# Decoder layer in split fp32: low weight parts at another address, and all high products of a stage ahead of the low ones

## The chip, the cores and the metric

The kernel runs on one core of a Trainium2 chip. The time is device microseconds of one execution, from the chip's own measurement; three runs of the kernel before took 1108.66 to 1108.97 us, median 1108.82. Beside them stands one execution that the hardware profiler recorded; its page and its trace are what is quoted here as the profile. On the page PE is TensorE (matmul), PEld its weight loads, DVE is VectorE, ACT ScalarE, POOL GpSimd, SP SyncE, which issues most DMAs.

## What is computed

One layer of a decoder over 256 rows of 2048 columns in float32: normalise, project to queries, keys and values of sixteen heads of 128, attend (eight heads with stick-breaking, eight with rotary and dilated windows), normalise each head, project back, add; then normalise, project up to 11008 columns, convolve over three rows, gate with GELU, project down, normalise and add.

```python
h = rmsnorm(x, pre_mix_gain)
proj = jnp.einsum('bsd,de->bse', h, w_in)
q_sb, k_sb, v_sb, q_dl, k_dl, v_dl = jnp.split(proj, splits, axis=-1)
o_sb = stick_breaking_attention(q_sb, k_sb, v_sb)              # 8 heads
o_dl = dilated_attention(rope(q_dl), rope(k_dl), v_dl)         # 8 heads
mixed = concat(head_rmsnorm(o_sb, sb_out_gain), head_rmsnorm(o_dl, dil_out_gain))
x = x + rmsnorm(mixed @ w_out, post_mix_gain)
h = rmsnorm(x, pre_ffn_gain)
u = causal_depthwise_conv(h @ w_up, conv_w, width=3) + conv_b
gate, val = jnp.split(u, 2, axis=-1)
x = x + rmsnorm((gelu(gate) * val) @ w_down, post_ffn_gain)
```

## The kernel before

**Split operands.** [...] A product is then high × high, high × low and low × high. `load` (L73) brings a weight chunk of 128 x 2048 from HBM in two halves of 128 x 1024 (tag `raw`, five buffers), issued on SP; `high` (L86, ScalarE, L88) and `low` (L91, VectorE, L93) write `wh` and `wl`, four buffers each, that is two chunks' worth. `split` (L82) does both for a chunk. `ahead` (L184) keeps loads two chunks ahead of the matmuls and splits one chunk ahead.

**The chunks** (L166 to L180) run in this order: values (`v`), and per head a query and a key chunk (`qk`), the output projection (`out`), then 43 gate and 43 value chunks of the up projection (`up`). The loop at L738 takes one chunk a turn; a turn is called a stage here, and it ends with `step()` (L910), which moves every head under way on by one piece of its attention, and with `down.presum` (L912), whose argument is the tick.

**Products of a `qk` or `up` chunk** are in `mm_stationary` (L96). The weights are the stationary operand. For each of the two halves come eight matmuls of a high part, moving 512 columns of `hT2` (256 high and 256 low columns of the activations, L101), then eight of a low part, moving the 256 high columns (L104); so a chunk runs eight high, eight low, eight high, eight low, all into one PSUM tile. The first two `up` chunks have their own order (`mm_stationary_late`, L106). Values, output and down hold the activations stationary and move 512 columns of weights (`mm_moving`, L133, and `Down.multiply`, L607).

**After the products** of an `up` chunk `convolved` (L486) adds the PSUM halves, scales by row, convolves and gates on VectorE and ScalarE. A `qk` chunk is added to `qk` (L776) and then used by `stick_head` (L366) or `dilated_head` (L394), generators whose pieces `step` runs a stage apart: scores `z`, exponentials, `spl` (L384) or the rotated `qk` (L400), products, and `finish_head` (L334).

**Presums.** `Down.presum` (L563) sums pairs of blocks of the down weights ahead of time, one pair per two ticks: at an even tick it loads `b12` and `t13` (L578, L580), at the odd tick after the next, three later, VectorE adds them (L574), and a tick after that the sum is stored to HBM (L569). `t13` has three buffers. All three DMAs are issued on SP, between the raw loads.

**Addresses.** On-chip memory is given out per partition in program order of the pools. In the compiled kernel before, `hT`, `raw`, `wh`, `wl`, `ident`, `x1`, `mix`, `qk`, `cv`, `yt`, `yp` and nearly every other large tile begin 384 bytes past a multiple of 512; slices of them are taken at multiples of 512 bytes. Small tiles (a few columns) lie in the pool `small` in steps of 32 bytes.

**Order.** The instructions of each engine are laid out by the framework's planner from priorities, dependencies and free buffers, except where the kernel pins them (`pin`, `keep_in_program_order`). [...]

Of the kernel before, what the change touches and what calls it, by code (L numbers as in the profile page):

```python
# [9 lines left out]
F32 = mybir.dt.float32  # L10
# [3 lines left out]
ALU = mybir.AluOpType  # L14
# [37 lines left out]
def layer_kernel(ctx: ExitStack, tc: tile.TileContext, a, out: bass.AP):  # L52
# [15 lines left out]
            tc.keep_in_program_order(ins)  # L68
        return ins

    HALF = 1024

    def load(src, w, piece=HALF):  # L73
        raws = []
# [4 lines left out]
            raws.append(raw)  # L79
        return raws  # L80

    def split(raws):  # L82

        return [low(raw, high(raw)) for raw in raws]

    def high(raw):  # L86
        wh = wpool.tile([P, raw.shape[1]], F32R, tag="wh", name="wh", bufs=4, padded_shape=[P, HALF])
        pin(A.copy(wh, raw))  # L88
        return wh

    def low(raw, wh):  # L91
        wl = wpool.tile([P, raw.shape[1]], F32R, tag="wl", name="wl", bufs=4, padded_shape=[P, HALF])
        pin(V.tensor_tensor(wl, raw, wh.bitcast(F32), op=ALU.subtract))  # L93
        return wh, wl

    def mm_stationary(ps, parts, h):  # L96

        for i, (wh, wl) in enumerate(parts):
            for j in range(8):
                k = 8 * i + j  # L100
                T.matmul(ps, wh[:, j * P:(j + 1) * P], h[:, k, :, :], start=(k == 0), stop=False, skip_group_check=True)  # L101
            for j in range(8):
                k = 8 * i + j
                T.matmul(ps[:, 0, :], wl[:, j * P:(j + 1) * P], h[:, k, 0, :], start=False, stop=(k == KT - 1), skip_group_check=True)  # L104
# [45 lines left out]

    def rstd_of(v, n):

        l = small.tile([P, n], F32, tag=f"rl{n}", name="rl")
        A.activation(l, v, AF.Ln)
        r0 = small.tile([P, n], F32, tag=f"r0{n}", name="r0")
        A.activation(r0, l, AF.Exp, scale=-0.5)
        q = small.tile([P, n], F32, tag=f"rq{n}", name="rq")
# [3 lines left out]
        r = small.tile([P, n], F32, tag=f"rr{n}", name="rr")  # L161
        V.tensor_tensor(r, r0, q, op=ALU.mult)
        return r

# [19 lines left out]
    def ahead(i, splits=SPLITS):  # L184
        if i + LOADS >= len(chunks):
            down.load(2 * (i + 1 + LOADS - len(chunks)))
        if i + 1 == len(chunks):
            down.prepare(2)
        while len(raws) < min(len(chunks), i + 1 + LOADS):
            j = len(raws)  # L190
            if j in between:
                nc.sync.dma_start(*between[j])
            raws[j] = load(chunks[j][3], chunks[j][4])
        while len(parts_of) < min(len(chunks), i + 1 + splits):
            j = len(parts_of)
            parts_of[j] = split(raws[j])
        return parts_of[i]


# [8 lines left out]
    phA = tc.tile_pool(name="phA", bufs=2)  # L208
    apool = phA.__enter__()
    cst = apool.tile([P, C_END - P], F32, name="cst", bufs=1)  # L210
    gpre = small.tile([P, KT], F32, name="gpre", bufs=1)
    x1 = apool.tile([P, 2, D], F32, name="x1", bufs=1)
    x1_kept = nc.dram_tensor("x1_kept", (S, D), F32, kind="Internal").ap()

# [33 lines left out]
    def split_block(g, k):  # L248
        c = slice(k % 2 * 512, k % 2 * 512 + 512)
        if k % 2 == 0:  # L250
            first[g] = [wpool.tile([P, HALF], F32R, tag=tag, name=tag, bufs=4) for tag in ("wh", "wl")]
# [30 lines left out]
    for i in range(1, 4):  # L282
        load_x(4 * i, 4 * i + 4)
        for j in range(2 * i, 2 * i + 2):
            raws[j] = load(chunks[j][3], chunks[j][4])
        split_x(4 * i, 4 * i + 4)
        if i == 1:
            parts_of[2] = split(raws[2])
# [12 lines left out]
    sinR = apool.tile([P, 2, S], F32, name="sinR", bufs=1)  # L301
    rstd1 = cpool.tile([P, 2], F32, name="rstd1", padded_shape=[P, 2 + 112])

    def along_rows(r, name):

        ps = ps_at.tile([P, S], F32, tag="at", name=name)
        for t in range(2):
            dg = small.tile([P, P], F32, tag="diag", name="diag", bufs=1)
            V.tensor_scalar(dg, ident, r[t], -1.0, op0=ALU.mult, op1=ALU.mult)
            T.matmul(ps[:, t * P:(t + 1) * P], negones, dg, start=True, stop=True)  # L310
        return ps

    def first_norm():

        V.tensor_copy(tri, cst[:, C_TRI:C_TRI + P])
        G.tensor_copy(idb, ident)
        G.tensor_copy(mskb, cst[:, C_MSK:C_MSK + P])
        ss = small.tile([P, 2], F32, tag="ssx", name="ssx", bufs=1)
        for t in range(2):
            A.activation(gbc, x1[:, t, :], AF.Square, accum_out=ss[:, t:t + 1])  # L320
        v0 = small.tile([P, 2], F32, tag="vx", name="vx", bufs=1)
        V.tensor_scalar(v0, ss, 1.0 / D, EPS, op0=ALU.mult, op1=ALU.add)
        V.tensor_copy(rstd1, rstd_of(v0, 2))
        rps = along_rows((rstd1[:, 0:1], rstd1[:, 1:2]), "rps")
        V.tensor_scalar(rB[:, 0, :], rps, SCALE, None, op0=ALU.mult)
        V.tensor_copy(rB[:, 1, :], rps)
        for s in range(2):
            V.tensor_tensor(cosR[:, s, :], cst[:, C_COS:C_COS + S], rB[:, s, :], op=ALU.mult)
            V.tensor_tensor(sinR[:, s, :], cst[:, C_SIN:C_SIN + S], rB[:, s, :], op=ALU.mult)
# [4 lines left out]
    def finish_head(h, at, den):  # L334
# [4 lines left out]
        T.matmul(po[:, 0, :], at[:, 0:P], vt[:, 0, hc], start=True, stop=True)  # L339
        T.matmul(po[:, 1, :], at[:, P:2 * P], vt[:, 0, hc], start=True, stop=False)  # L340
        T.matmul(po[:, 1, :], at[:, 2 * P:3 * P], vt[:, 1, hc], start=False, stop=True)
        hs = small.tile([P, 2], F32, tag="hs", name="hs")
        for t in range(2):
            jk = apool.tile([P, P], BF16, tag="jk", name="jk")
            A.activation(jk, po[:, t, :], AF.Square, accum_out=hs[:, t:t + 1])
        v = small.tile([P, 2], F32, tag="hv", name="hv")
        if den is None:
            V.tensor_scalar(v, hs, 1.0 / P, EPS, op0=ALU.mult, op1=ALU.add)
        else:

            e2 = small.tile([P, 2], F32, tag="e2", name="e2")
# [42 lines left out]
    def dilated_head(h, qk):  # L394
# [9 lines left out]
        T.matmul(z[:, 0:P], qk[:, 0, 0:P], qk[:, 1, 0:P], start=True, stop=True)  # L404
        T.matmul(z[:, P:3 * P], qk[:, 0, P:S], qk[:, 1, :], start=True, stop=True)
        sm = apool.tile([P, 3 * P], F32, tag="t15", name="sm", bufs=3)
        m = small.tile([P, 2], F32, tag="m", name="m")
        den = small.tile([P, 2], F32, tag="den", name="den")
# [50 lines left out]
    def second_norm():  # L459

        rs = [sq.newton(*sq.mean(t)) for t in range(2)]
        r2B = cpool.tile([P, S], F32, name="r2B")
        V.tensor_scalar(r2B, along_rows(rs, "r2ps"), -0.5, None, op0=ALU.mult)
        return r2B


# [53 lines left out]
    class Down:  # L520
# [217 lines left out]
    for i, (kind, p, s, _, w) in enumerate(chunks):  # L738
# [40 lines left out]
        elif kind == "out":  # L779
# [14 lines left out]
            else:  # L794
# [40 lines left out]
                for t in range(2):  # L835
# [8 lines left out]
                    if t == 0:  # L844
                        for c in range(4):
                            update(0, c)
                        hs = [high(raw) for raw in raws[i + 1]]
                        up0.append(low(raws[i + 1][0], hs[0]))
# [12 lines left out]
                    highs(b)  # L861
                hs.append(high(raws[i + 2][1]))
                update(1, 3)
                up0.append(low(raws[i + 1][1], hs[1]))
                parts_of[i + 1] = up0
                for b in range(4, 6):
                    turn(1, b)
# [12 lines left out]
                square(1, 2, 3)  # L880
                lows(2)
                lows(3)
                parts_of[i + 2] = [low(raws[i + 2][0], hs[2])]
                for b in range(4, 8):
                    lows(b)
                parts_of[i + 2].append(low(raws[i + 2][1], hs[3]))
                parts_of[i + 3] = [low(raw, h) for raw, h in zip(raws[i + 3], hs[4:])]
                keep(0)
                keep(1)
                pinned[0] = False  # L890
# [102 lines left out]
```

## Time and profile before

| | before |
|---|---|
| median of three runs | 1108.82 us |
| the profiled execution | 1108.83 us |
| its span, first to last instruction | 1107.0 us |
| granted TensorE clock, mean | 0.997 |
| PE busy | 1095.9 us |
| PEld busy | 942.7 us |
| DVE busy | 879.1 us |
| ACT busy | 661.3 us |
| mean DMA rate | 233 GB/s |

The stretches of the span, read off the starts of the groups: values and query/key with the attention to about 304 us, the output projection and the second norm to about 400, up from 400 to 885, down from 885 on. In a row of the timeline stand the start, the time from there to the last end, engine, line, operation, out<-in, shape and count; neighbours of one kind are merged. In a row of groups stand the count, busy time and mean duration in ns of one, and the idle time before them. A matmul's duration is longer than its distance from the next, since matmuls are pipelined: distances are read from starts.

### The profile page before, as it was taken

To read this page: it belongs to the slowest core of one execution; us is meant where nothing else is said; L and a number is where in the kernel's file an instruction comes from. 1 tells how busy PE (TensorE), PEld (TensorE's weight loads), DVE (VectorE), ACT (ScalarE), POOL (GpSimd) and SP (SyncE) were. 2 spreads that over 40 slices of the span, in tenths; PEclk is the share of its full clock that TensorE was granted. 3 is DMA by queue.
4 is the path that set the end of the run, shared out by engine and by line. 5 is a ranking of instruction groups with operands and counts; after the bars stand their busy time and mean duration, and the time that the engine had idled before them with its cause. 6 is when DMAs were issued, how large, how long until landed. Compare 5 with 4: busy or idle time off the path is not lost.

```text
span 1107.0 us, 16307 instructions
## 1 busy us (share of the span) xinstructions
PE 1095.9 (99%) x5855; PEld 942.7 (85%) x5855; DVE 879.1 (79%) x1371; ACT 661.3 (60%) x1046; POOL 5.3 (0%) x12
## 2 busy tenths in 40 slices
PE   9999999999999999999999999999999999999996
PEld 6888888888888888888888888888888888888885
DVE  6577776777776589888888888888888898889887
ACT  6656664655654376656565555555556566666665
POOL 0000000000000000000000000000000000000001
PEclk9999999999999999999999999999999999999998
DMA  8977778878879856666555556556555577767775
GB/s 317 382 257 272 257 246 281 296 253 285 271 260 318 276 196 215 193 190 190 185 192 183 189 187 190 188 190 190 191 188 190 170 253 244 258 217 255 242 246 210
DMA packets 75393, 257.79 MB, mean 233 GB/s; under 512 B 8496, under 2 KB 9520, under 8 KB 74544
## 3 DMA queue, kind: packets, MB, share of 16 engines
q1 hardware_dynamic: 74880, 256.22, 69.5%
q8 instruction: 46, 0.75, 0.3%
q10 hardware_dynamic: 432, 0.53, 0.1%
q14 instruction: 35, 0.29, 0.1%
HBM read 238.89 MB, written 17.83 MB: 232 GB/s over the span
## 4 chain that ended last, share of the span: by engine, by line
PE 97%; DMA 1%; DVE 0%; ACT 0%; SPq 0%; issue 0%; DVEq 0%; ACTq 0%
PE mmu L101 28%; PE mmu L104 14%; PE mmqk L101 11%; PE p L622 7%; PE p L620 7%; PE p L621 7%; PE mmqk L104 6%; PE mmo L147 3%; PE mmo L143 3%; PE mmo L144 3%; PE mmv L147 2%; PE mmv L143 2%; PE mmv L144 2%; PE mmu L110 1%; DMA mg<-in_xT 1%; DMA raw<-in_w_v 0%
## 5 line engine op out<-in xcount | busy, mean ns | idle before, releaser
L88 ACT CAST wh<-raw 128x1024 fp32r<-128x1024 f32 (+1 forms) x408 | 414.6, 1024 | 348.3 <-PE mmu L101 186.6
L93 DVE TENSOR_TENSOR wl<-raw,wh 128x1024 fp32r<-128x1024 f32 (+1 forms) x408 | 482.3, 1188 | 159.2 <-ACT wh L88 147.9
L101 PE MATMUL mmu<-hT,wh 128*128 128x512 f32 x1344 | 336.8, 392 | 0.0
L101 PEld LDWEIGHTS mmu<-hT,wh 128*128 128x128 f32 x1344 | 241.7, 189 | 43.1
L104 PEld LDWEIGHTS mmu<-hT,wl 128*128 128x128 f32 x1344 | 183.4, 190 | 13.1
L104 PE MATMUL mmu<-hT,wl 128*128 128x256 f32 x1344 | 187.6, 282 | 0.0
L101 PE MATMUL mmqk<-hT,wh 128*128 128x512 f32 x512 | 131.7, 398 | 0.0
L101 PEld LDWEIGHTS mmqk<-hT,wh 128*128 128x128 f32 x512 | 92.2, 189 | 16.7
L104 PEld LDWEIGHTS mmqk<-hT,wl 128*128 128x128 f32 x512 | 69.8, 190 | 5.1
L104 PE MATMUL mmqk<-hT,wl 128*128 128x256 f32 x512 | 71.4, 282 | 0.0
L622 PE MATMUL p<-wl,yp 128*128 128x512 f32 x182 | 70.9, 390 | 0.0
L620 PE MATMUL p<-wh,yp 128*128 128x512 f32 x182 | 70.8, 389 | 0.0
L621 PE MATMUL p<-wh,yp 128*128 128x512 f32 x182 | 70.8, 389 | 0.0
L621 PE MATMUL p<-wh,yt 128*128 128x512 f32 (+1 forms) x140 | 53.6, 383 | 0.0
L620 PE MATMUL p<-wh,yt 128*128 128x512 f32 (+1 forms) x140 | 53.6, 383 | 0.0
L622 PE MATMUL p<-wl,yt 128*128 128x512 f32 (+1 forms) x140 | 53.4, 383 | 0.0
L493 ACT ACTIVATE cv<-u,par 128x256 f32<-128x256 f32 x86 | 51.4, 597 | 2.5 <-DVE u L491 2.3
L143 PE MATMUL mmv<-wh,hT 128*128 128x512 f32 x128 | 51.0, 400 | 0.0
L143 PE MATMUL mmo<-wh,mix 128*128 128x512 f32 x128 | 50.4, 394 | 0.0
L144 PE MATMUL mmv<-wh,hT 128*128 128x512 f32 x128 | 50.2, 392 | 0.2 <-DVE hT L228 0.2
L88 ACT CAST wh<-room 128x1024 fp32r<-128x1024 f32 x26 | 27.4, 1053 | 38.1 <-PE p L621 35.7
L144 PE MATMUL mmo<-wh,mix 128*128 128x512 f32 x128 | 49.8, 389 | 0.0
(178 smaller groups left out, 1221.2 us busy)
## 6 DMA issues: line engine op xcount, KB each, us to landing
raw<-in_w_up SPq DMA_DIRECT2D x172, 512.0 KB, 4.3
raw<-in_w_qk SPq DMA_DIRECT2D x64, 512.0 KB, 5.2
raw<-in_w_dn SPq DMA_DIRECT2D x60, 512.0 KB, 4.5
raw<-in_w_o SPq DMA_DIRECT2D x32, 512.0 KB, 5.1
raw<-in_w_v SPq DMA_DIRECT2D x28, 512.0 KB, 5.6
t<-in_w_dn SPq DMA_DIRECT2D x26, 512.0 KB, 5.7
t_kept<-t SPq DMA_DIRECT2D x26, 512.0 KB, 3.9
raw<-t_kept SPq DMA_DIRECT2D x26, 512.0 KB, 4.4
```

The lines of the kernel that those rows point to most:

```text
L88: pin(A.copy(wh, raw))
L93: pin(V.tensor_tensor(wl, raw, wh.bitcast(F32), op=ALU.subtract))
L101: T.matmul(ps, wh[:, j * P:(j + 1) * P], h[:, k, :, :], start=(k == 0), stop=False, skip_group_check=True)
L104: T.matmul(ps[:, 0, :], wl[:, j * P:(j + 1) * P], h[:, k, 0, :], start=False, stop=(k == KT - 1), skip_group_check=True)
L110: T.matmul(ps[:, part, :], parts[k // 8][low][:, k % 8 * P:(k % 8 + 1) * P], h[:, k, part, :], skip_group_check=True, **kw)
L143: T.matmul(ps[t], hi[:, k, tc_], ws, start=(first and i == 0 and j == 0), stop=False)
L144: T.matmul(ps[t], lo[:, k, tc_], ws, start=False, stop=False)
L147: T.matmul(ps[t], hi[:, k, tc_], wl[:, j * 512:(j + 1) * 512], start=False, stop=(last and i == len(parts) - 1 and j == n - 1))
L493: A.activation(cv, u, AF.Identity, scale=cw(2), bias=par[:, P_CB + f:P_CB + f + 1])
L620: T.matmul(ps, yh, wh[:, cs], start=key not in self.begun, stop=False)
L621: T.matmul(ps, yl, wh[:, cs], start=False, stop=False)
L622: T.matmul(ps, yh, wl[:, cs], start=False, stop=self.left[key] == 0)
```

## The change

- `low` takes the kind of the chunk. Each `wl` buffer is 512 bytes longer (`HALF + P` columns). For kinds `qk` and `up` the low part begins 80 columns, 320 bytes, into its buffer; for the others it begins at 0 as before. All `wl` buffers share a tag, so the four buffers still begin at the same place modulo 512.
- `mm_stationary` multiplies the high parts of both halves first, sixteen matmuls, then the low parts of both, sixteen. The products are the same ones.
- Small tiles of `rstd_of`, `finish_head` and `dilated_head` move from the pool `small` to the pool `apool`, with the same four buffers. `gpre` is padded by 128 bytes.
- `along_rows` takes its two diagonal matrices side by side in one tile from its caller (tag `half` of `apool` in the first norm, tag `pair` of `phB` in the second) in place of one `diag` tile used twice.
- `Down.presum` adds a pair at the even tick two after its loads, ahead of the next pair's loads, and stores it at the tick after that; `t13` has two buffers in place of three.

```diff
-    HALF = 1024
+    HALF, LOW_AT = 1024, 80
...
-    def low(raw, wh):
-        wl = wpool.tile([P, raw.shape[1]], F32R, tag="wl", name="wl", bufs=4, padded_shape=[P, HALF])
+    def low(raw, wh, kind=None):
+
+        at = LOW_AT if kind in ("qk", "up") else 0
+        wl = wpool.tile([P, at + raw.shape[1]], F32R, tag="wl", name="wl", bufs=4, padded_shape=[P, HALF + P])[:, at:]
         pin(V.tensor_tensor(wl, raw, wh.bitcast(F32), op=ALU.subtract))
         return wh, wl
 
     def mm_stationary(ps, parts, h):
 
-        for i, (wh, wl) in enumerate(parts):
+        for i, (wh, _) in enumerate(parts):
             for j in range(8):
                 k = 8 * i + j
                 T.matmul(ps, wh[:, j * P:(j + 1) * P], h[:, k, :, :], start=(k == 0), stop=False, skip_group_check=True)
+        for i, (_, wl) in enumerate(parts):
             for j in range(8):
                 k = 8 * i + j
                 T.matmul(ps[:, 0, :], wl[:, j * P:(j + 1) * P], h[:, k, 0, :], start=False, stop=(k == KT - 1), skip_group_check=True)
...
-        l = small.tile([P, n], F32, tag=f"rl{n}", name="rl")
+        l = apool.tile([P, n], F32, tag=f"rl{n}", name="rl", bufs=4)
...
-    gpre = small.tile([P, KT], F32, name="gpre", bufs=1)
+    gpre = small.tile([P, KT], F32, name="gpre", bufs=1, padded_shape=[P, KT + 32])
...
-    def along_rows(r, name):
+    def along_rows(r, name, dg):
 
         ps = ps_at.tile([P, S], F32, tag="at", name=name)
         for t in range(2):
-            dg = small.tile([P, P], F32, tag="diag", name="diag", bufs=1)
-            V.tensor_scalar(dg, ident, r[t], -1.0, op0=ALU.mult, op1=ALU.mult)
-            T.matmul(ps[:, t * P:(t + 1) * P], negones, dg, start=True, stop=True)
+            V.tensor_scalar(dg[:, t, :], ident, r[t], -1.0, op0=ALU.mult, op1=ALU.mult)
+            T.matmul(ps[:, t * P:(t + 1) * P], negones, dg[:, t, :], start=True, stop=True)
         return ps
...
-        rps = along_rows((rstd1[:, 0:1], rstd1[:, 1:2]), "rps")
+        dg = apool.tile([P, 2, P], F32, tag="half", name="diag", bufs=1)
+        rps = along_rows((rstd1[:, 0:1], rstd1[:, 1:2]), "rps", dg)
...
-        hs = small.tile([P, 2], F32, tag="hs", name="hs")
+        hs = apool.tile([P, 2], F32, tag="hs", name="hs", bufs=4)
...
-        V.tensor_scalar(r2B, along_rows(rs, "r2ps"), -0.5, None, op0=ALU.mult)
+        dg = phB.tile([P, 2, P], F32, tag="pair", name="diag", bufs=1, padded_shape=[P, 7, P])
+        V.tensor_scalar(r2B, along_rows(rs, "r2ps", dg), -0.5, None, op0=ALU.mult)
...
-            if not odd and 0 <= pair - 2 < len(self.presums):
-                t13, _, kept = self.summed[pair - 2]
+            if odd and 0 <= pair - 1 < len(self.presums):
+                t13, _, kept = self.summed[pair - 1]
                 tc.keep_in_program_order(nc.sync.dma_start(kept, t13))
-            if odd and 0 <= pair - 1 < len(self.presums):
+            if not odd and 0 <= pair - 1 < len(self.presums):
                 t13, one, _ = self.summed[pair - 1]
...
-                t13 = apool.tile([P, HALF], F32, tag="t13", name="t13", bufs=3)
+                t13 = apool.tile([P, HALF], F32, tag="t13", name="t13", bufs=2)
```

More of the change, by code (lines that the diff above doesn't have):

```diff
@@ L80, in load, with split @@
         return raws
-    def split(raws):
-        return [low(raw, high(raw)) for raw in raws]
+    def split(raws, kind):
+        return [low(raw, high(raw), kind) for raw in raws]
     def high(raw):
@@ L151, in rstd_of @@
     def rstd_of(v, n):
-        l = small.tile([P, n], F32, tag=f"rl{n}", name="rl")
+        l = apool.tile([P, n], F32, tag=f"rl{n}", name="rl", bufs=4)
         A.activation(l, v, AF.Ln)
-        r0 = small.tile([P, n], F32, tag=f"r0{n}", name="r0")
+        r0 = apool.tile([P, n], F32, tag=f"r0{n}", name="r0", bufs=4)
         A.activation(r0, l, AF.Exp, scale=-0.5)
-        q = small.tile([P, n], F32, tag=f"rq{n}", name="rq")
+        q = apool.tile([P, n], F32, tag=f"rq{n}", name="rq", bufs=4)
         V.tensor_tensor(q, r0, r0, op=ALU.mult)
@@ L160, in rstd_of @@
         V.tensor_scalar(q, q, -0.5, 1.5, op0=ALU.mult, op1=ALU.add)
-        r = small.tile([P, n], F32, tag=f"rr{n}", name="rr")
+        r = apool.tile([P, n], F32, tag=f"rr{n}", name="rr", bufs=4)
         V.tensor_tensor(r, r0, q, op=ALU.mult)
@@ L195, in ahead @@
             j = len(parts_of)
-            parts_of[j] = split(raws[j])
+            parts_of[j] = split(raws[j], chunks[j][0])
         return parts_of[i]
@@ L250, in split_block @@
         if k % 2 == 0:
-            first[g] = [wpool.tile([P, HALF], F32R, tag=tag, name=tag, bufs=4) for tag in ("wh", "wl")]
+            first[g] = [wpool.tile([P, HALF], F32R, tag=tag, name=tag, bufs=4, padded_shape=[P, n]) for tag, n in (("wh", HALF), ("wl", HALF + P))]
         wh, wl = (w[:, c] for w in first[g])
@@ L287, in layer_kernel @@
         if i == 1:
-            parts_of[2] = split(raws[2])
+            parts_of[2] = split(raws[2], chunks[2][0])
     tc.keep_in_program_order(nc.sync.dma_start(ident, a["cst"][:, C_ID:C_END]))
@@ L345, in finish_head @@
             A.activation(jk, po[:, t, :], AF.Square, accum_out=hs[:, t:t + 1])
-        v = small.tile([P, 2], F32, tag="hv", name="hv")
+        v = apool.tile([P, 2], F32, tag="hv", name="hv", bufs=4)
         if den is None:
@@ L349, in finish_head @@
         else:
-            e2 = small.tile([P, 2], F32, tag="e2", name="e2")
+            e2 = apool.tile([P, 2], F32, tag="e2", name="e2", bufs=4)
             V.scalar_tensor_tensor(e2, den, EPS, den, op0=ALU.mult, op1=ALU.mult)
@@ L406, in dilated_head @@
         sm = apool.tile([P, 3 * P], F32, tag="t15", name="sm", bufs=3)
-        m = small.tile([P, 2], F32, tag="m", name="m")
-        den = small.tile([P, 2], F32, tag="den", name="den")
+        m = apool.tile([P, 2], F32, tag="m", name="m", bufs=4)
+        den = apool.tile([P, 2], F32, tag="den", name="den", bufs=4)
         for t, cs in ((0, slice(0, P)), (1, slice(P, 3 * P))):
@@ L847, in layer_kernel @@
                         hs = [high(raw) for raw in raws[i + 1]]
-                        up0.append(low(raws[i + 1][0], hs[0]))
+                        up0.append(low(raws[i + 1][0], hs[0], "up"))
                         hs.append(high(raws[i + 2][0]))
@@ L863, in layer_kernel @@
                 update(1, 3)
-                up0.append(low(raws[i + 1][1], hs[1]))
+                up0.append(low(raws[i + 1][1], hs[1], "up"))
                 parts_of[i + 1] = up0
@@ L882, in layer_kernel @@
                 lows(3)
-                parts_of[i + 2] = [low(raws[i + 2][0], hs[2])]
+                parts_of[i + 2] = [low(raws[i + 2][0], hs[2], "up")]
                 for b in range(4, 8):
                     lows(b)
-                parts_of[i + 2].append(low(raws[i + 2][1], hs[3]))
-                parts_of[i + 3] = [low(raw, h) for raw, h in zip(raws[i + 3], hs[4:])]
+                parts_of[i + 2].append(low(raws[i + 2][1], hs[3], "up"))
+                parts_of[i + 3] = [low(raw, h, "up") for raw, h in zip(raws[i + 3], hs[4:])]
                 keep(0)
```

## The prediction

> **What bounds the kernel.** I read the page first: its span, its busy rows and its chain of work that ended last.
>
> ```profile
> span 1107.0 us, 16307 instructions
> PE 1095.9 (99%) x5855; PEld 942.7 (85%) x5855; DVE 879.1 (79%) x1371; ACT 661.3 (60%) x1046; POOL 5.3 (0%) x12
> ...
> PE 97%; DMA 1%; DVE 0%; ACT 0%; SPq 0%; issue 0%; DVEq 0%; ACTq 0%
> ...
> L101 PE MATMUL mmu<-hT,wh 128*128 128x512 f32 x1344 | 336.8, 392 | 0.0
> L104 PE MATMUL mmu<-hT,wl 128*128 128x256 f32 x1344 | 187.6, 282 | 0.0
> L101 PE MATMUL mmqk<-hT,wh 128*128 128x512 f32 x512 | 131.7, 398 | 0.0
> L104 PE MATMUL mmqk<-hT,wl 128*128 128x256 f32 x512 | 71.4, 282 | 0.0
> ```
>
> TensorE carries 97% of the chain, so a change is worth what it does to the spacing of matmuls. The edited function issues the last four groups. A stage is 16 high matmuls of 512 columns and 16 low ones of 256, now in the order 8, 8, 8, 8. There are 1344/16 = 84 stages in up and 512/16 = 32 in query/key, **116** in all, with 116 × 16 = **1856** low matmuls. The profiled execution took 1108.83 us, 1.8 us more than its span, and the median of the three runs is 1108.82, so the sum holds for both.
>
> The next view is the PE timeline of one stage in up; the first column is the start.
>
> ```profile
> 501.97 2.00 PE L101 MATMUL mmu<-hT,wh 128*128 128x512 f32 x8
> 503.81 1.12 PE L104 MATMUL mmu<-hT,wl 128*128 128x256 f32 x8
> 504.76 2.00 PE L101 MATMUL mmu<-hT,wh 128*128 128x512 f32 x8
> 506.61 1.11 PE L104 MATMUL mmu<-hT,wl 128*128 128x256 f32 x8
> 507.56 2.00 PE L101 MATMUL mmu<-hT,wh 128*128 128x512 f32 x8
> 509.40 1.12 PE L104 MATMUL mmu<-hT,wl 128*128 128x256 f32 x8
> 510.35 0.86 PE L101 MATMUL mmu<-hT,wh 128*128 128x512 f32 x3
> ```
>
> Ends are modelled, so I use starts. Eight highs take 1.84, 1.85 and 1.84 us (mean 1.843), eight lows 0.95 each time, a stage 507.56 − 501.97 = 5.59. Narrower windows of the same timeline give the spacing inside a run of lows (the first row starts with the second low, the next with the seventh), then the down stage, whose matmuls are all 512 wide and listed singly.
>
> ```profile
> 503.93 0.40 PE L104 MATMUL mmu<-hT,wl 128*128 128x256 f32 x2
> 504.52 0.40 PE L104 MATMUL mmu<-hT,wl 128*128 128x256 f32 x2
> 949.73 0.39 PE L621 MATMUL p<-wh,yp 128*128 128x512 f32 x1
> ...
> 952.90 0.39 PE L620 MATMUL p<-wh,yp 128*128 128x512 f32 x1
> ```
>
> From the second low to the seventh are five spacings in 0.59, and from the seventh to the next run (504.76) two in 0.24: **0.12 us** each. The first low takes 0.11 to 0.12 (503.81 to 503.93); by the run's total it is 0.95 − 7 × 0.12 = 0.11. The down stage has 14 spacings in 3.17: **0.2264** for a steady 512-column matmul. Eight steady ones would take 1.811, so a run of highs that follows lows loses 1.843 − 1.811 = 0.032 at its start.
>
> A steady 0.12 for 256 columns and 0.2264 for 512 differ by 0.106, which is what 256 columns cost; the remainder, 0.013 to 0.014, is paid once per matmul in both. One weight load runs beside each matmul in both, and in the addresses of the compiled kernel both streams, `hT` and weights, begin 384 bytes past a multiple of 512. So the remainder may be a collision of the two reads, and it depends on their phase: the first lows and first highs of a run differ from the later ones with the same addresses.
>
> **The order of the products.** One run of 16 and 16 loses one start of highs (0.032) and one short first low (0.01). Highs: 1.843 + 8 × 0.2264 = 3.654. Lows: 0.95 + 8 × 0.12 = 1.91. Together 5.564 against 5.587, 0.023 less, times 116 = **2.6 us** gained, certain as far as the rows go.
>
> **The address of the low parts.** No row of before has the two reads 320 bytes apart, so the steady low is bounded from both sides. [...]
>
> ```profile
> 203.81 0.49 PE L418 MATMUL ptw<-ident,sm 128*128 128x128 f32 x3
> L418 PE MATMUL ptw<-ident,sm 128*128 128x128 f32 x24 | 3.9, 272 | 0.0
> ```
>
> Three in 0.49 with 0.272 for one: (0.49 − 0.272) / 2 = **0.109**, 0.011 under the steady low. Above, by the worst spacing of highs. These are the second and the seventh high of the run that begins at 504.76, and the durations of all lows in up.
>
> ```profile
> 505.00 0.62 PE L101 MATMUL mmu<-hT,wh 128*128 128x512 f32 x2
> 506.15 0.62 PE L101 MATMUL mmu<-hT,wh 128*128 128x512 f32 x2
> L104 PE MATMUL mmu<-hT,wl x1344: 277/283/364, 413.7 to 881.7; 128*128 128x256 f32 x192
> ```
>
> The six spacings before the seventh take 506.15 − 504.76 = 1.39, 0.2317 each, 0.0053 over the steady ones; the first alone is 505.00 − 504.76 = 0.24, some 0.01 over. A bad phase thus costs 0.005 on average and 0.01 at worst, and the low could go to 0.125, at the extreme to 0.13. Between 0.109 and 0.13 I take **0.113**. Minimum and median of that last row are 277 and 283 ns: the shortest low lies 6 ns under the usual one (0.12 − 0.006 = 0.114), and by starts the first low of a run was 0.11. That is a phase which these matmuls have shown, and the steady 0.12 is nearly the worst they show. A stage is then 3.654 + 16 × 0.113 = 5.462, 0.125 less than now; times 116 is **14.5 us**, and 1108.8 − 14.5 = **1094.3**.
>
> [...]
>
> **What else is edited.** Who waits for whom, of PE, ACT and DVE, the busy times of the up stage, and the DMAs of the presums, from issue to landing:
>
> ```profile
> PE idle L236 <- DVE warm L233: 1.2, 1, 1.2
> ACT wh L88 <- PE mmu L101: 186.6, 164, 1.7
> DVE diag L309 <- PE rps L310: 3.6, 1, 3.6
> 412.00:885.00 473.00, 473.00 (x2707) 415.92 (x2706) 395.05 (x650) 280.46 (x424) 0.00 (x0) 1.00 0.59 190
> t<-in_w_dn SPq DMA_DIRECT2D x26, 512.0 KB, 5.7
> t_kept<-t SPq DMA_DIRECT2D x26, 512.0 KB, 3.9
> ```
>
> TensorE's longest wait of the whole run is 1.2 us, at the start, and casts wait for TensorE to free buffers, not the reverse. So the second `wh`, now needed eight lows (0.95) earlier, comes in time. VectorE works 395.05 of 473 us there (83.5%); if that stretch shrinks like the stage, by 0.125/5.587, to 462, it is at 85.5% and still not the bound. The copy of row `[128, 2, 128]` in place of one reused `diag` removes DVE's 3.6 us wait; TensorE was not held by it, so nothing. The presum's add moves one tick (one stage) earlier: its operand has two ticks, 10.9 us, and lands in 5.7. Its store is issued at the next odd tick, and with two buffers instead of three the load that reuses the buffer comes one tick, 5.46, after it; the store lands in 3.9. On SP the raw loads queue behind that load, with 1.5 us to spare before they are late, and ACT's casts, which wait for TensorE, hide that. If the cover were gone, 24 reuses at up to 1 us each could show, which I count as unlikely. The tiles moved between pools change only addresses: nothing.
>
> **Rivals.**
>
> *The floor*: the collision vanishes and lows run at 0.109. The stage is 3.654 + 1.744 = 5.398, 0.189 less, 21.9 us: **1086.9**. [...]
>
> *No effect of the address*: the remainder is a fixed price of these matmuls. Only the order counts: 1108.8 − 2.6 = **1106.2**. For it speaks that the remainder is equal at 256 and 512 columns; against, that the first low has less of it.
>
> *Low buffers come free later*: the first `wl` buffer of a stage is released after 24 products instead of 16. A DVE queue that keeps its order would stand at that `wl`, and attention operands behind it would reach TensorE late. Two places of the query/key stage, DVE first, PE after:
>
> ```profile
> 152.25 1.23 DVE L93 TENSOR_TENSOR wl<-raw,wh 128x1024 fp32r<-128x1024 f32 x1
> 153.40 0.55 DVE L384 TENSOR_TENSOR spl<-sp,sph 128x384 fp32r<-128x384 f32 x1
> 155.11 0.33 PE L387 MATMUL z<-spl,tri 128*128 128x384 f32 x1
> 208.22 1.22 DVE L93 TENSOR_TENSOR wl<-raw,wh 128x1024 fp32r<-128x1024 f32 x1
> 209.36 0.68 DVE L400 TENSOR_TENSOR qk<-qk,rot 128x512 f32<-128x512 f32 x1
> 210.40 0.39 PE L404 MATMUL z<-qk 128*128 128x128 f32 x2
> 204.06 2.09 PE L101 MATMUL mmqk<-hT,wh 128*128 128x512 f32 x8
> 149.04 2.09 PE L101 MATMUL mmqk<-hT,wh 128*128 128x512 f32 x8
> 150.97 1.11 PE L104 MATMUL mmqk<-hT,wl 128*128 128x256 f32 x8
> ```
>
> The stage that starts at 149.04 would free that buffer at 149.04 + 1.93 + 1.81 + 0.90 = 153.68; `wl` and `spl` then end near 155.46, and TensorE wants `spl` at about 154.98: 0.5 us late. By the same sum from 204.06, the start of its stage, `qk` is done at 210.6 and wanted at 210.27: 0.3 late. Eight heads of each kind: 8 × 0.5 + 8 × 0.3 = 6.4 us given back, **1100.7**. It needs the low part to stay ahead in DVE's order, which is laid out anew.
>
> *Slower: a worse phase.* If 320 bytes apart costs the lows what the first highs pay, 0.0053, they run at 0.1253; the stage is 3.654 + 2.005 = 5.659, 0.072 more, 8.4 us: **1117.2** (1126 at 0.13). It decides from (5.587 − 3.654) / 16 = 0.1208 on: a steady low above that makes the kernel slower. For it speaks that all reads now share one residue and the first highs show phases that cost more; against, that lows have not shown one clearly above 0.12.
>
> **How the numbers follow.** Main case 0.38, floor 0.18, no effect 0.16, late buffers 0.10, worse phase 0.18. The measurement tells about 0.2% (2.2 us) from no change. The main case, the floor and the late buffers are faster by more; 1106.2 lies at that border, half to each side: faster 0.74, same 0.08, slower 0.18. The range leaves out only the worse phase: from 1084 (floor, and the 0.023 per stage lost at a run's start gone a second time) to 1108 (the address nothing, and the order a third of its sum). Forecast **1094.3**.
>
> **What would show it.** In the PE timeline of the changed kernel a run of 16 highs should take 3.65 us, and 16 lows 1.81; 1.74 means the floor, 1.91 no effect, 2.0 a worse phase. Late buffers would show as PE waits on DVE at `spl` or `qk` and DVE waits of `wl` on PE. The highs' spacing should stay 0.2264; if it moves, the low parts' address also touches the run after them and the sum is wrong by up to 0.03 × 116 = 3.5 us.

## The result and the profile after

| | before | changed |
|---|---|---|
| median | 1108.89 us (4 runs, 1108.66 to 1109.27) | 1103.17 us (4 runs, 1102.63 to 1103.41) |
| ratio of the runs, 95% interval | | 0.9947 [0.9934, 0.9960] |
| span of the profiled execution | 1107.0 us | 1101.5 us |

The change gains 5.7 us, where 14.5 were forecast. The page of the changed kernel shows the same picture as before: TensorE carries the chain, and the two groups of `mm_stationary` in up (now L103 and L107) are its largest.

```profile
span 1101.5 us, 16267 instructions
PE 1089.8 (99%) x5855; PEld 940.5 (85%) x5855; DVE 872.3 (79%) x1371; ACT 668.0 (61%) x1046; POOL 5.3 (0%) x12
...
PE 96%; DMA 1%; ACT 1%; DVE 0%; issue 0%; SPq 0%; DVEq 0%; ACTq 0%
...
L103 PE MATMUL mmu<-hT,wh 128*128 128x512 f32 x1344 | 320.7, 391 | 0.0
L107 PE MATMUL mmu<-hT,wl 128*128 128x256 f32 x1344 | 172.4, 281 | 0.0
```

The PE timeline of the changed kernel, in up, is the view that answers to the one of before; the first column is the start.

```profile
499.79 3.81 PE L103 MATMUL mmu<-hT,wh 128*128 128x512 f32 x16
503.44 2.05 PE L107 MATMUL mmu<-hT,wl 128*128 128x256 f32 x16
505.33 3.81 PE L103 MATMUL mmu<-hT,wh 128*128 128x512 f32 x16
508.98 2.05 PE L107 MATMUL mmu<-hT,wl 128*128 128x256 f32 x16
510.87 3.81 PE L103 MATMUL mmu<-hT,wh 128*128 128x512 f32 x16
```

Sixteen highs take 503.44 − 499.79 = 3.65 us, as the sum had it. Sixteen lows take 505.33 − 503.44 = 1.89, **0.118 each**, where 1.81 and 0.113 were forecast. A stage is 5.54 instead of 5.587; 0.047 × 116 stages = 5.4 us, beside 5.5 between the spans. The product takes up's stage for those of query/key too. From the starts of the first matmul of each stretch in the two traces, the query/key stretch is 1.9 us shorter and the up stretch, from its third chunk on, 3.8 (84 × 0.047 = 3.9). So the gain lies in these two stretches, and nearly the whole miss in one number, the spacing of a low.

The last view of the changed kernel is who waits for whom: PE's longest two waits, two of DVE's, and one of SP's queue (us in total, times, longest).

```profile
PE idle L239 <- DVE warm L236: 1.2, 1, 1.2
PE pth L824 <- DVE x L816: 1.2, 1, 1.2
...
DVE wl L95 <- PE mmqk L107: 8.6, 13, 0.7
DVE wl L95 <- PE mmu L107: 5.4, 28, 0.8
...
SPq L584 <- DMA t_kept<-t: 42.7, 23, 3.7
```

VectorE does now wait for low buffers that TensorE frees later, and SP does wait for the store of a presum before it reloads the buffer, 42.7/23 = 1.9 us each time on average. Neither reaches TensorE: its waits are those of before, but for one of 0.4 us on an operand of the first projection.

### The profile page after: what moved, and what is told of

It reads as the page before. It is cut to its first block, busy times and chain, and to the rows that moved or that the text cites. A ratio compares the mean times of both kernels' runs of the same rounds, so it can differ in the third digit from the quotient of the medians.

```text
span 1101.5 us, 16267 instructions
## 1 busy us (share of the span) xinstructions
PE 1089.8 (99%) x5855; PEld 940.5 (85%) x5855; DVE 872.3 (79%) x1371; ACT 668.0 (61%) x1046; POOL 5.3 (0%) x12
## 4 chain that ended last, share of the span: by engine, by line
PE 96%; DMA 1%; ACT 1%; DVE 0%; issue 0%; SPq 0%; DVEq 0%; ACTq 0%
PE mmu L103 28%; PE mmu L107 14%; PE mmqk L103 11%; PE p L626 7%; PE p L625 7%; PE p L624 7%; PE mmqk L107 5%; PE mmo L147 3%; PE mmo L146 3%; PE mmo L150 3%; PE mmv L150 2%; PE mmv L146 2%; PE mmv L147 2%; DMA mg<-in_xT 1%; PE mmu L113 1%; DMA raw<-in_w_v 0%
## 5 line engine op out<-in xcount | busy, mean ns | idle before, releaser
L88 ACT CAST wh<-raw 128x1024 fp32r<-128x1024 f32 (+1 forms) x408 | 413.0, 1024 | 250.9 <-PE mmu L103 118.2
L95 DVE TENSOR_TENSOR wl<-raw,wh 128x1024 fp32r<-128x1024 f32 (+1 forms) x408 | 475.7, 1187 | 90.7 <-ACT wh L88 51.4
L103 PE MATMUL mmu<-hT,wh 128*128 128x512 f32 x1344 | 320.7, 391 | 0.0
L103 PEld LDWEIGHTS mmu<-hT,wh 128*128 128x128 f32 x1344 | 246.9, 188 | 47.7
L107 PEld LDWEIGHTS mmu<-hT,wl 128*128 128x128 f32 x1344 | 170.2, 189 | 6.4
L107 PE MATMUL mmu<-hT,wl 128*128 128x256 f32 x1344 | 172.4, 281 | 0.0
L103 PE MATMUL mmqk<-hT,wh 128*128 128x512 f32 x512 | 125.3, 396 | 0.0
L103 PEld LDWEIGHTS mmqk<-hT,wh 128*128 128x128 f32 x512 | 94.4, 188 | 18.9
L498 DVE SCALAR_TENSOR_TENSOR cv<-u,par,cv 128x255 f32<-128x255 f32 x86 | 41.6, 483 | 68.7 <-ACT cv L497 68.6
L107 PEld LDWEIGHTS mmqk<-hT,wl 128*128 128x128 f32 x512 | 64.8, 189 | 2.4
L107 PE MATMUL mmqk<-hT,wl 128*128 128x256 f32 x512 | 65.5, 281 | 0.0
L131 ACT COPY half<-mmu 128x256 f32<-128x256 f32 x86 | 32.0, 372 | 41.9 <-PE mmu L107 38.7
L88 ACT CAST wh<-room 128x1024 fp32r<-128x1024 f32 x26 | 27.4, 1053 | 38.8 <-PE p L625 37.0
```

Source lines behind the costliest of these rows:

```text
L498: V.scalar_tensor_tensor(cv[:, 1:], u[:, :S - 1], cw(1), cv[:, 1:], op0=ALU.mult, op1=ALU.add)
```

## The experiments

Every kernel below is the changed kernel with the edit shown. Spacings in ns are distances between the starts of neighbouring matmuls of one stage, read from the trace. Times of timed runs are medians, with the kernel before run on the same chip. A low and a high are a matmul of a low and of a high part: ScalarE writes the high part as an fp32r cast of the weights (`wh`, L88 of the changed kernel), VectorE the low part as the difference of weights and high part (`wl`, L95).

### The order alone, and the address alone

```diff
-    HALF, LOW_AT = 1024, 80
+    HALF, LOW_AT = 1024, 0
```

> The changed kernel with the low parts at the start of their buffers again, 0 bytes further; everything else of the change is kept. Theory A (both parts count: a run of highs after lows costs 0.027 us less often, and the other phase makes a low 0.118 instead of 0.120): lows steady at 0.120, 16 highs in 3.65 us, 1106.2 to 1106.6 us, 2.3 to 2.6 under before. Theory B (the order is the whole gain and the address does nothing): 1103.2, as the changed kernel.

Measured: **1106.18 us** (9 runs) beside 1108.81, ratio 0.9976 [0.9966, 0.9985]. Its PE timeline in up:

```profile
500.35 3.82 PE L103 MATMUL mmu<-hT,wh 128*128 128x512 f32 x16
504.00 2.08 PE L107 MATMUL mmu<-hT,wl 128*128 128x256 f32 x16
505.91 3.82 PE L103 MATMUL mmu<-hT,wh 128*128 128x512 f32 x16
```

Highs 3.65, lows 1.91: theory B falls, and the time is 2.6 us lower, to the tenth what the prediction's sum gave the order. In part that is luck: by the starts a stage in up takes 5.567 on average, 0.020 under before, which is 1.7 us over 84 stages; the rest is in the query/key stretch, 1.1 us shorter in the trace, whose stages also hold the attention's matmuls. The second kernel puts the order back:

```diff
-        for i, (wh, _) in enumerate(parts):
+        for i, (wh, wl) in enumerate(parts):
...
-        for i, (_, wl) in enumerate(parts):
             for j in range(8):
```

> The changed kernel with eight high, eight low, eight high, eight low again; the low parts stay 320 bytes further. Theory A: eight lows take 0.943 us instead of 0.952 (0.118 each, and the short first low of a run is gone), eight highs 1.84 as before: 2 x 0.009 x 116 = 2 us under before, 1106.9. Theory B: as before, 1108.9. A third outcome, 1104 or less, would say that the two parts help each other not at all and the address is nearly everything.

Measured: **1105.85 us** (8 runs) beside 1108.81, ratio 0.9973 [0.9962, 0.9983]. Its timeline:

```profile
500.63 2.00 PE L103 MATMUL mmu<-hT,wh 128*128 128x512 f32 x8
502.47 1.11 PE L106 MATMUL mmu<-hT,wl 128*128 128x256 f32 x8
503.41 2.00 PE L103 MATMUL mmu<-hT,wh 128*128 128x512 f32 x8
505.25 1.11 PE L106 MATMUL mmu<-hT,wl 128*128 128x256 f32 x8
506.19 2.00 PE L103 MATMUL mmu<-hT,wh 128*128 128x512 f32 x8
```

A stage is 506.19 − 500.63 = 5.56. The address alone gains 3.0 us, one more than expected (eight highs after these lows take 1.837 us, where before had 1.841, and eight lows 0.943 in place of 0.953). 2.6 and 3.0 make 5.6 beside the 5.7 of the whole change: the parts add up. Both kernels keep the moved tiles and the other presum order of the change, which no run tries by themselves; since they are in both sums, the sum of 5.6 leaves them about nothing. What is missing is missing in the address: 3.0 measured, 14.5 − 2.6 = 11.9 forecast.

### What sets the spacing of a low: the address?

```diff
-        at = LOW_AT if kind in ("qk", "up") else 0
+        at = 8 * (lows_at[0] // 2 % 16) if kind == "up" else 0
+        lows_at[0] += kind == "up"
```

> In up the low parts lie at another place in each chunk, 0, 32, 64 ... 480 bytes further in turn, in query/key at 0. Looked at is the steady spacing of the lows of each chunk. Theory A (collision of the two reads, which depends on their phase): the spacing differs by offset, 0.120 at 0, 0.118 at 320, and somewhere between 0.109 and 0.117. Theory C (a fixed price of some 0.011 us for each such matmul, the address moving it by a cycle or two only): 0.117 to 0.121 at every offset.

> In up the low parts lie 192, 196, 200 ... 252 bytes further in turn, in query/key 192. The coarse sweep had 0.1178 at 192 and 0.1168 at 224. Theory C2: every step stays between 0.1165 and 0.121, the best at 224 or beside it. A place under 0.114 would say that the collision can be dodged after all, and the fixed price falls.

The fine sweep has `at = 48 + lows_at[0] // 2 % 16`. Mean spacing of the lows in ns, by bytes of displacement (from the starts in the traces of the two runs, some 75 to 90 distances each, the first ones of a run included):

```
coarse   0: 119.7   32: 118.3   64: 117.7   96: 117.3  128: 120.4  160: 119.7  192: 117.8  224: 116.8
       256: 119.5  288: 118.3  320: 117.8  352: 117.3  384: 120.4  416: 119.7  448: 117.8  480: 116.8
fine   204: 122.6  208: 116.6  212: 117.3  216: 118.9  220: 121.1  224: 116.8  240: 117.3  252: 119.1
```

The pattern repeats every 256 bytes, not 512. Every place lies between 116.6 and 122.6, none near 109 or 113. At this point a fixed price of each such matmul (theory C) looked likely, though the fine sweep went beyond what C2 allowed (122.6 at 204, 121.1 at 220) and had its best place at 208, not at 224. The highs answer in the same way:

```diff
+        at = 8 * (highs_at[0] // 2 % 16) if kind == "up" else 0
+        highs_at[0] += kind == "up"
+        wh = wpool.tile([P, at + raw.shape[1]], F32R, tag="wh", name="wh", bufs=4, padded_shape=[P, HALF + P])[:, at:]
```

> Low parts at 0 everywhere; in up the HIGH parts lie 0, 32, 64 ... 480 bytes further in turn. Looked at is the spacing of highs of 512 columns by offset. Theory C2 (a fixed price of 0.010 us or more for each matmul, and 0.003 to 0.004 us that hang on the phase, as the sweep of the lows showed): 0.224 to 0.230, with the same repeat every 256 bytes. Theory D (highs have slack in the load, so that the address moves only the start of a run): 0.2264 at every offset.

Measured, mean spacing of highs including the start of a run: 228.5 at 0 and 228.9 at 192, 232.3 to 234.0 at the other places of this sweep, again with a repeat of 256 bytes. Theory D falls, and most places lie above the 224 to 230 of C2. None of these places is better for the highs than no displacement.

### Or the weight load?

In the next two kernels half of the weight columns are loaded, for highs and for lows in turn:

```diff
-                T.matmul(ps, wh[:, j * P:(j + 1) * P], h[:, k, :, :], start=(k == 0), stop=False, skip_group_check=True)
+                n = P if k == 0 else m
+                T.matmul(ps[0:n], wh[:, j * P:j * P + n], h[:, k, :, :], start=(k == 0), stop=False, skip_group_check=True)
```

> In every second pair of up chunks, fifteen of the sixteen high matmuls load 64 of the 128 weight columns (rows 64 to 127 of those products are left incomplete); they still move 512 columns. Looked at is the steady spacing of those highs beside the full ones. Theory A (the remainder over the moving columns is paid while a load is read): it is halved, 0.2264 becomes 0.219 to 0.221. Theory C (a fixed price of each matmul): 0.2264 unchanged.

```diff
-                T.matmul(ps[:, 0, :], wl[:, j * P:(j + 1) * P], h[:, k, 0, :], start=False, stop=(k == KT - 1), skip_group_check=True)
+                T.matmul(ps[0:m, 0, :], wl[:, j * P:j * P + m], h[:, k, 0, :], start=False, stop=(k == KT - 1), skip_group_check=True)
```

> The changed kernel, but in every second pair of up chunks the low matmuls load 64 of the 128 weight columns (rows 64 to 127 of those products are left out); they still move 256 columns. Looked at is the steady spacing of those lows. If a low waits for its weight load (0.109 of 0.118), half a load brings it down to 0.107 or less of moving plus the price of a matmul, 0.110 to 0.113. If it is the moving columns and a fixed price of the matmul that take the time, it stays at 0.117 to 0.120.

Highs with half loads do not get nearer to 220 ns: their median is 230 (full ones in the same run: 227), slower by 3 ns, which neither theory had. For the lows, the timeline of the second kernel; the first two rows are a run with half loads (`128*64`) and the run after it, the next two a run with full loads.

```profile
503.25 2.06 PE L107 MATMUL mmu<-hT,wl 128*64 128x256 f32 x16
505.14 3.83 PE L103 MATMUL mmu<-hT,wh 128*128 128x512 f32 x16
...
514.38 2.05 PE L107 MATMUL mmu<-hT,wl 128*128 128x256 f32 x16
516.26 2.00 PE L103 MATMUL mmu<-hT,wh 128*128 128x512 f32 x8
```

1.89 against 1.88 us: half a load (135 ns each in the profile, against 189 for a full one) did not shorten a low. So these lows did not wait for their loads, as the expectation's first case had it, and nothing here shows 0.109, read from 128-column matmuls, as their bound. The 0.107 of moving in that case was an estimate; no run shows the moving of 256 columns apart. Whether the bf16 form does better:

```diff
+                w, m = (wl[:, j * P:(j + 1) * P], h[:, k, 0, :])
+                if short:
+                    nb = negones.bitcast(BF16)
+                    w, m = nb[:, 0:P], nb[:, 0:S]
+                T.matmul(ps[:, 0, :], w, m, start=False, stop=(k == KT - 1), skip_group_check=True)
```

> In every second pair of up chunks the low matmuls multiply constants in bf16, 128 weight columns and 256 moving columns as before (their low products are left out). Looked at is the steady spacing of those lows. If the price of 0.010 us over the moving columns belongs to the four-byte form of matmul, they run at 0.107 to 0.110; if every matmul that follows a weight load pays it, 0.117 to 0.120.

Measured: median distance 109 ns for the bf16 matmuls and 118 for the fp32r lows of the same run. No fp32r low of any run here kept to 109 (the fastest sixteen, further down, take 1.81 us, 113 each). What lies above 109 thus goes with the four-byte operands or with their places: the bf16 matmuls read weights and moving columns from one small tile, again and again. Weights, moving columns and places were not tried apart.

### Two rhythms at one address

The run with narrow highs held a line that fits no fixed price: at 320 bytes, with full loads, its lows ran at two speeds. In its timeline the run of highs at 471.73 has full loads, the one at 477.27 half loads behind a full first one (the merged row names the first).

```profile
471.73 3.82 PE L104 MATMUL mmu<-hT,wh 128*128 128x512 f32 x16
475.38 2.05 PE L108 MATMUL mmu<-hT,wl 128*128 128x256 f32 x16
477.27 3.84 PE L104 MATMUL mmu<-hT,wh 128*128 128x512 f32 x16
480.95 2.00 PE L108 MATMUL mmu<-hT,wl 128*128 128x256 f32 x16
482.78 3.39 PE L104 MATMUL mmu<-hT,wh 128*128 128x512 f32 x14
```

After full highs sixteen lows take 1.89, after narrow highs 1.83, at one address and with the same loads. Theory E: the lows fall into a rhythm that keeps itself up, there is more than one at an address, and what ran before chooses. Two kernels keep the address of the lows that are looked at (320 bytes in the first, 64 in the second) and change what runs ahead of them: the lows of the first half, or the highs of the second half.

```diff
+        if kind == "up":
+            at = 2 * (lows_at[0] // 2 % 32) if lows_at[0] % 2 == 0 else LOW_AT
+            lows_at[0] += 1
```

> In up the low parts of the second half of each chunk stay 320 bytes further; those of the first half lie 0, 8, 16 ... 248 bytes further in turn. So lows nine to sixteen of a run all have the address of the changed kernel, and enter it from 32 different rhythms. Looked at is the spacing of lows ten to sixteen. Theory E (at one address the lows settle into one of several rhythms that keep themselves up, and what ran before chooses which; in the run with narrow highs they kept to 0.1133 at this very address): for some of the 32 they run at 0.113 to 0.114, for the others at 0.1177. Theory C2 (the address alone sets the spacing, and the half loads did it in the other run): 0.1177 for all 32.

```diff
+        if kind == "up":
+            at = 2 * (highs_at[0] // 2 % 32) if highs_at[0] % 2 else 0
+            highs_at[0] += 1
```

> All lows of query/key and up 64 bytes further (320 less the repeat of 256, where the sweep had the same spacings), in up the HIGH parts of the second half of each chunk 0, 8, 16 ... 248 bytes further in turn. Looked at is the sum of the sixteen lows that follow. Theory E: 1.82 to 1.84 us after some highs, 1.887 after the others. Theory C2: 1.887 throughout. The last eight highs cost 0.232 to 0.234 where they are displaced, 0.2264 at 0.

From the first of the two, two stages: with the first half at 64 bytes (highs from 620.58) and at 88 (highs from 637.23).

```profile
620.58 3.81 PE L106 MATMUL mmu<-hT,wh 128*128 128x512 f32 x16
624.24 2.05 PE L110 MATMUL mmu<-hT,wl 128*128 128x256 f32 x16
626.12 3.82 PE L106 MATMUL mmu<-hT,wh 128*128 128x512 f32 x16
...
637.23 3.81 PE L106 MATMUL mmu<-hT,wh 128*128 128x512 f32 x16
640.88 2.00 PE L110 MATMUL mmu<-hT,wl 128*128 128x256 f32 x16
642.71 1.55 PE L106 MATMUL mmu<-hT,wh 128*128 128x512 f32 x6
```

The sixteen distances behind these rows, in ns, with those of a stage of the kernel with the order alone (0 bytes) for comparison; lows nine to sixteen of the second and third line have one address:

```
  0 |   0 : 113 119 120 120 120 120 120 120 | 120 120 120 120 120 120 120 120
 64 | 320 : 118 117 118 118 118 118 117 118 | 118 117 118 118 118 118 118 120
 88 | 320 : 121 116 119 118 113 113 114 113 | 114 113 113 114 113 113 114 113
```

For 24 of the 32 places of the first half the second half ended in the rhythm of 113, for the other 8 in that of 118; stages of one place agreed with each other to 2 ns in a distance. The second kernel, after highs displaced by 56 bytes (from 632.59) and by 64 (from 638.13):

```profile
632.59 3.88 PE L107 MATMUL mmu<-hT,wh 128*128 128x512 f32 x16
636.31 1.98 PE L111 MATMUL mmu<-hT,wl 128*128 128x256 f32 x16
638.13 3.87 PE L107 MATMUL mmu<-hT,wh 128*128 128x512 f32 x16
641.83 2.05 PE L111 MATMUL mmu<-hT,wl 128*128 128x256 f32 x16
643.72 3.87 PE L107 MATMUL mmu<-hT,wh 128*128 128x512 f32 x16
```

In it 12 of the 31 displacements of the highs put the lows after them into the fast rhythm (sixteen in 1.81 to 1.84 us), the others and no displacement left them at 1.88 to 1.89. Each of the twelve costs the highs something, 0.02 to 0.065 us, against 0.05 to 0.07 that it brings the lows, which leaves between nothing and 0.04 us a stage; six of the other displacements cost the highs nothing, where 0.232 to 0.234 was expected for all. Theory E holds, theories C and C2 fall: nothing in the form of these matmuls or in the address of the changed kernel forbids 0.113. It is entered, or not.

### Faster versions

The changed kernel again, and four that use the above, each on one chip with its kernel before.

> The changed kernel once more, on the chip of the next three: 1103.2, 5.6 us under before.

`LOW_AT = 52`, 208 bytes:

> The changed kernel with the low parts of query/key and up 208 bytes further instead of 320. The fine sweep had a steady low of 0.1166 at 208, against 0.1178 at 320: 0.0011 x 1856 = 2.1 us under the changed kernel, 1101.1, if a place that was swept with other places beside it keeps its spacing when all lows lie there. If neighbours matter, between 1101 and 1104.

The same, with the order of the two runs turned in every second up chunk:

```diff
+        for n, run in enumerate((lows, highs) if low_first else (highs, lows)):
+            run(n == 0, n == 1)
```

> As the one at 208 bytes, and every second up chunk runs its sixteen lows ahead of its sixteen highs, so that runs of highs and of lows of neighbouring chunks join. Half of the starts of highs after lows go, 42 of 84: 42 x 0.027 = 1.1 us under the one at 208, 1100.0. If the low parts come too late for that (they are needed 3.65 us sooner), PE waits for DVE at wl appear and the time is above 1101.

`LOW_AT = 22`, 88 bytes:

> The changed kernel with all low parts of query/key and up 88 bytes further instead of 320. In the run that swept the first half, lows at 88 entered the fast rhythm by the fifth (0.121, 0.116, 0.119, 0.118, then 0.1133). Theory E, if 88 keeps that rhythm for all sixteen: 16 lows in 1.834 us instead of 1.887, highs unchanged: 0.053 x 116 = 6.2 us under the changed kernel, 1096.9. If 88 falls back into a slow rhythm after the eighth: about 1101.

Both places, one for each half:

```diff
+    HALF, LOW_AT, n_low = 1024, (22, 80), [0]
...
+            at = LOW_AT[n_low[0] % 2]
+            n_low[0] += 1
```

> As the changed kernel, but the low parts of the first half of each chunk 88 bytes further, of the second half 320, in query/key and up. In the sweep this pair gave 0.927 + 0.907 = 1.834 us for sixteen lows, against 1.887. Theory E: 1096.9, 6.2 us under the changed kernel, faster than every kernel so far. Theory C2 (the address alone sets the spacing): not under 1101.

| kernel | median us | beside before | ratio, 95% interval |
|---|---|---|---|
| changed, again | 1102.95 | 1108.92 | 0.9947 [0.9933, 0.9960] |
| 208 bytes | 1099.60 | 1108.92 | 0.9916 [0.9903, 0.9930] |
| 208 bytes, turned | 1099.15 | 1108.92 | 0.9912 [0.9898, 0.9925] |
| 88 bytes | 1097.41 | 1109.30 | 0.9893 [0.9879, 0.9908] |
| 88, then 320 bytes | **1097.00** | 1109.30 | 0.9890 [0.9874, 0.9907] |

The PE timeline of the last, in up:

```profile
502.60 3.81 PE L106 MATMUL mmu<-hT,wh 128*128 128x512 f32 x16
506.26 2.00 PE L110 MATMUL mmu<-hT,wl 128*128 128x256 f32 x16
508.09 3.81 PE L106 MATMUL mmu<-hT,wh 128*128 128x512 f32 x16
```

Lows 1.83, a stage 5.49, as the expectation had it: the fast rhythm holds over a whole kernel and is worth what its spacing says. Lows at 208 keep a mean of 117 without the fast rhythm. That kernel beat its expectation by 1.5 us: after those lows sixteen highs take 3.640 us in place of 3.653, and 0.013 × 116 = 1.5. So turning every second chunk had less to gain than the 1.1 us expected: a run of 32 highs takes 7.267 where two of sixteen take 7.280, some 0.5 us over the kernel. No wait of TensorE for `wl` appeared, but the interval does not tell this kernel from the one not turned. The last two do not differ beyond their intervals either.

## Why the prediction was wrong

- **Order of the products**: 2.6 us forecast, 2.6 measured without the address. Sixteen highs in one run take 3.65 us where two runs of eight took 2 × 1.841, so some 0.03 for one start of highs is gone from a stage; the rows of before gave the size of the whole (0.023 a stage forecast, 0.020 measured in up). That the total agrees to the tenth is in part luck, as said above.
- **Address of the low parts**: the direction was right, the term was mis-sized. The failed step is "Between 0.109 and 0.13 I take **0.113**", with its reason that "That is a phase which these matmuls have shown". They had shown it in the first low of a run, once, on the way from one steady state to another. The steady low became 0.1177, so it gained 2.3 ns and not 7, and since the short first low went too, sixteen lows gained 1.91 − 1.89 = 0.02 us; the stage took 5.54 where 5.462 was forecast. With the measured spacing the prediction's own sum is right: 3.654 + 16 × 0.118 = 5.542, 0.045 × 116 = 5.2 us.
- **What the runs showed in its place**: 0.113 is a steady state too, at the very address of the change, but the run of highs ahead of it leads into the other one. The prediction treated the spacing as a property of the address and asked nothing about how it is reached. Two kernels that lead into it come to 1097.4 and 1097.0, some 3 us from the forecast 1094.3. The last of them gains 1109.3 − 1097.0 = 12.3 us, against 14.5: its first four lows of a run still take 116 to 121 ns, so sixteen take 1.83 us and not 1.81. Why there are two such states was not found.
- **The bounds**: 0.109, which the floor's 1.744 multiplies by 16, is the spacing of three plain fp32 transposes of 128 columns, one load each. That it is the time of a load, or a bound for a low, no run shows: the profile of before lists the loads of these transposes (L418, PEld) at 140 ns each, and half a load did not shorten a low (1.89 us for sixteen, against 1.88). What the runs showed in its place are steady spacings of 0.113 for fp32r lows and 0.109 for bf16 ones. The upper end, 0.125 to 0.13, was reached at no place tried; the slowest, 204 bytes, had 0.1226.
- **No effect of the address**: 1106.2 was its forecast, and that is where the kernel without displacement stands (1106.18); with it the time is 3 us lower, and over the places tried a low takes 116.6 to 122.6 ns. So the address matters here. Why it does is not shown by any run. A collision of two reads was the author's conjecture: a repeat of 256 bytes was measured, but sixteen lows with half loads took 1.89 us against 1.88 with full ones, where a collision proportional to the load would have made them shorter.
- **Late buffers**: the waits came (`DVE wl L95 <- PE`, 8.6 us for `mmqk` and 5.4 for `mmu`), and none was passed on to TensorE.
- **What else is edited**: nothing showed on the path. But the spare time on SP was misjudged: it waits 42.7 us for stores of presums, where the sum had 1.5 us to spare each time. The cover, casts that wait for TensorE and not for loads, held as said: in up they still wait 118.2 us for `mmu`.

## What to carry to other kernels

The spacing seen once at the edge of a run was not the steady one here: 113 ns for the first low of a run, 120 from the third on (0 bytes). Before such a number is multiplied by 1856, ask which state the run will settle into and what leads there. Where matmuls of one shape run at different spacings (lows here at 116.6 to 122.6 ns, by their place), sweep the place of an operand inside one kernel, a different one for each block, and read the spacings by block: one run gave 16 or 32 places, and stages of one place agreed to about a nanosecond in the mean. And sweep what runs ahead of a block as well: lows at 320 bytes ran at 113 or at 118 ns here, by the place of the lows ahead of them.

## What the runs showed of the hardware that was not expected

- One address, two rhythms: sixteen fp32r lows of 256 columns ran at 113.3 or 117.7 ns with operands of the same form at the same places, by what ran just ahead, and once in a rhythm kept to it until the run ended.
- The place of the stationary operand moves a 256-column fp32r matmul between 116.6 and 122.6 ns and a 512-column one between 228.5 and 234.0 (starts of runs included), with a repeat of 256 bytes and differences from 4 bytes on (122.6 at 204, 116.6 at 208).
- bf16 matmuls of 256 columns ran at 109 ns in the same place of the same kernel. The row of the highs behind them looks longer by 0.1 us:

```profile
507.61 1.92 PE L111 MATMUL mmu<-negones 128*128 128x256 bf16 x16
509.29 3.91 PE L103 MATMUL mmu<-hT,wh 128*128 128x512 f32 x16
513.04 2.05 PE L111 MATMUL mmu<-hT,wl 128*128 128x256 f32 x16
```

The highs from 509.29 take 513.04 − 509.29 = 3.75, against 3.65 in the changed kernel. But in narrower windows of this timeline the last bf16 low starts at 509.26, only 0.03 ahead of the first high, and the second high at 509.60. From the last low to the second high are 0.34 us, which is what a low of 0.109 and a first high of 0.233 make. Thus 0.08 of the 0.1 us is the place of one start in the records, and the highs lose some 0.02. So a start at the border of two kinds of matmul is best read together with its neighbours.
